# A latent-attention layer in split fp32: scores from two full-height products and one of half height, rotated queries computed in the z stage, a shorter inverse root

## The chip, the cores and the metric

The program runs on one core of a Trainium2 chip. The metric is the device time of one execution in microseconds. Each core has a matrix engine (PE; its weight loads are shown as PEld), a vector engine (DVE), a scalar engine (ACT), GpSimd (POOL) and a queue engine that issues DMAs (SP). The core works from an on-chip memory of 128 partitions; products of PE land in accumulator banks (PSUM), from which DVE and ACT read them.

## The reference, cut to what matters

One layer of multi-head latent attention with a gated output and a per-layer embedding. There are 1024 tokens, 16 heads, 64 plain and 32 rotated query and key features for each head; all heads share one rotated key.

```python
u = h @ w_in
c_q, c_kv, k_rope, z = jnp.split(u, ...)
q = (rmsnorm(c_q, q_norm) @ w_q_b).reshape(B, S, MLA_HEADS, MLA_NOPE + MLA_ROPE)
q_rope = apply_rope(q[..., MLA_NOPE:], cos, sin)
k_rope = apply_rope(k_rope, cos, sin)
s = (einsum('bqhd,bkhd->bhqk', q_nope, k_nope) + einsum('bqhd,bkd->bhqk', q_rope, k_rope)) * scale
prob = softmax(where(k_chunk <= q_chunk, s, -inf))
o = einsum('bhqk,bkhd->bqhd', prob, v)
y = (o * silu(z)) @ w_out
x = x + y
x = x + sigmoid(rmsnorm(x) @ ple_gate) * (p @ ple_proj)
return rmsnorm(x, final_norm)
```

## The kernel before, in words

All values are fp32. PE works on a reduced fp32 form, so each operand is split into a rounded part (`hi`) and the rest (`lo`), and a product is the sum of three: hi·hi, hi·lo and lo·hi. ACT usually makes `hi` by a copy, and DVE or POOL makes `lo` by a subtraction (`sub_hi`, L91).

The stages follow each other. The u stage computes the compressed queries, keys and the raw rotated key for eight tiles of 128 tokens. The z stage (loop over `c`, L513) computes the gate path in eight column blocks of 48 products each; beside it run the last two transposes of u, the rotated key (`rope_key`), the tables of cosines and sines spread over the partitions (`rope_tables`, `cs`) and the query parts of the first four heads (`project_r`). The attention stage loops over 16 heads times 8 blocks of 128 queries in the order `ORDER`; block `i` sees `n = 128 (i+1)` keys. A head has scores (L609), a row maximum on DVE (L614), an exponential on ACT (L619), transposes of the probabilities on PE (L121), the split of these (L650, L91), and the product with the values (L661). Blocks are in flight together: transposes come two blocks behind the scores, values four. For each pair of heads `project_q` and `project_k` (L423, L553) compute queries and keys; for each four heads `project_v` computes values, and `project_r` the query parts that carry the rotation. Calls of these stand at fixed block numbers (`K_AT`, `Q_AT`, `R_AT`, `V_AT`); within them a scheduler sets the order on each engine when the program is built, and engines work in that order. The last stage is the output product, the gate and the embedding (L751), with an inverse root (`rsqrt`, L93) on one column for each tile.

In the scores of before, an array row is one of 128 features: 64 plain ones, 32 query features times cosine, and 32 times sine, against keys arranged to match (`k_hi`, `k_lo`). Each block is three products of the full 128 rows over all its keys, in pieces of up to 512 columns. `project_r` multiplies by the cosine and the sine separately, splits the result and writes both parts to memory outside the core; `rope_q` reads the rows of each head back. The keys of an odd head are copied by DVE to `kst` and split later by ACT and POOL (`odd_k`).

Of the kernel before, what the change touches and what calls it, by code (L numbers as in the profile page):

```python
# [40 lines left out]
V_AT, K_AT, Q_AT, R_AT = (4, 4, 2, 2), (0, 3), (6, 7), (1, 6)  # L41
# [10 lines left out]
def mla_ple_kernel(ctx, tc, x, x_t, p_t, pos, norm_g, w_c, w_z, q_norm, w_q, w_r, kv_norm, w_k, w_v,  # L52
# [338 lines left out]
    cs = [att1.tile([P, S], F32, name=f"cs{e}") for e in range(2)]  # L391
    att2 = late.enter_context(pool("att2", side="right"))
    k_hi, k_lo = zip(*([att2.tile([P, S], F32R, name=f"k_{z}{e}") for z in ("hi", "lo")] for e in range(2)))

    def load_split(src, cols, name, bufs):
# [3 lines left out]
        hi = att1.tile([P, n], F32R, tag=name + "h", name=name + "h", bufs=bufs)  # L399
        lo = att1.tile([P, n], F32R, tag=name + "l", name=name + "l", bufs=bufs)  # L400
        G.tensor_copy(out=hi, in_=stg)
        sub_hi(G, lo, stg, hi)
        return tuple(z.rearrange("p (k n) -> p k n", k=cols[0]) for z in (hi, lo))

    wk_of, wv_of, wq_of, wr_of, q_of, rq_of = {}, {}, {}, {}, {}, {}

    def weights(h):
        if h >= H:
            return
        if h % 4 == 0:  # L410
            wr_of[h // 4] = load_split(w_r[h // 4], (QL // P, P), "wr", 1)
# [15 lines left out]
    def project_r(g, hf):  # L427

        cols = slice(hf * 512, hf * 512 + 512)
        if hf == 0:  # L430
            rq_of[g] = [tc.dram_tile([2, P, S], F32, name=f"rq{g}{z}") for z in "hl"]
        ps = product_q(wr_of[g], hf)
        t = rt_tile("rt").rearrange("p (c n) -> p c n", c=2)
        for n in range(2):
            V.tensor_tensor(out=t[:, n, :], in0=ps, in1=cs[n][:, cols], op=ALU.mult)
        hi = rh_tile("rh").rearrange("p (c n) -> p c n", c=2)
        lo = t.bitcast(F32R)
        A.copy(out=hi, in_=t)
        sub_hi(G, lo, t, hi)
        for z, d in zip((hi, lo), rq_of[g]):  # L440
            nc.gpsimd.dma_start(out=d.rearrange("c p n -> p c n")[:, :, cols], in_=z.bitcast(F32))

    def token_rows(name, src, n):

        blk = rh_tile(name + "b").bitcast(F32)[:, :NT * n]
# [9 lines left out]

    def rope_key():
# [3 lines left out]
        k1, k2 = kr[:, :, :HF], kr[:, :, HF:ROPE]  # L462
        for dst, a, b, op in ((k1, cosT, sinT, ALU.subtract), (k2, sinT, cosT, ALU.add)):
# [3 lines left out]
        V.tensor_copy(out=kr[:, :, ROPE:ROPE + HF], in_=k2)  # L467
        V.tensor_scalar(out=kr[:, :, ROPE + HF:], in0=k1, scalar1=-1.0, scalar2=None, op0=ALU.mult)
        kt = rt_tile("kt")
        d = token_rows("kt", kr, 2 * ROPE)  # L470
        for e in range(2):
            nc.gpsimd.dma_start(out=kt[e * NOPE:(e + 1) * NOPE, :], in_=d)
        for e in range(2):
            rows = slice(NOPE * (1 - e), NOPE * (2 - e))
            A.copy(out=k_hi[e][rows], in_=kt[rows])
            sub_hi(V, k_lo[e][rows], kt[rows], k_hi[e][rows])

    def rope_tables():
        for tab, src, name in zip(cs, (cosT, sinT), ("cos", "sin")):
            t = rt_tile("spread")[:, :NT * 32].rearrange("p (t n) -> p t n", t=NT)  # L480
            V.tensor_copy(out=t.rearrange("p t (m n) -> p t m n", n=HF),
                          in_=src.unsqueeze(2).broadcast_to([P, NT, 32 // HF, HF]))
            d = token_rows(name, t, ROPE)
# [17 lines left out]
    zw = zph.enter_context(pool("zw", reuse_waits="tile"))  # L501

    for c in range(KT):
# [13 lines left out]
        A.activation(out=zT[:, c, :], in_=zT[:, c, :], func=AF.Silu)  # L517
        if c < 2:
            u_transposes(*pend.pop(0))
        if c == 1:  # L520
            rope_key()
        if c == 2:
            rope_tables()
        if c == 3:
            weights(0)
        if c in (4, 5):
            project_r(0, c - 4)
# [14 lines left out]
    kst = att.tile([P, S], F32, name="kst")  # L542
# [4 lines left out]
    def project_k(c, hf):  # L547
# [7 lines left out]
        A.copy(out=k_hi[0][:NOPE, cols], in_=ps[:NOPE])  # L555
        V.tensor_copy(out=kst[NOPE:, cols], in_=ps[NOPE:])
        sub_hi(V, k_lo[0][:NOPE, cols], ps[:NOPE], k_hi[0][:NOPE, cols])
# [20 lines left out]
    def rope_q(h):  # L578
        q_of[h] = [att.tile([P, S], F32R, tag="q" + z, name="q" + z, bufs=3) for z in "hl"]
        r0 = NOPE * (1 - h % 2)  # L580
        for z, d in zip(q_of[h], rq_of[h // 4]):
            for n in range(2):
                nc.sync.dma_start(out=z[r0 + n * ROPE:r0 + (n + 1) * ROPE, :].bitcast(F32),
                                  in_=d[n, h % 4 * ROPE:(h % 4 + 1) * ROPE, :])

    def project_q(c, hf):
        cols = slice(hf * 512, hf * 512 + 512)
        ps = product_q(wq_of[c], hf)
        for e in range(2):
            rows = slice(e * NOPE, (e + 1) * NOPE)  # L590
            hi, lo = q_of[2 * c + e]
            A.copy(out=hi[rows, cols], in_=ps[rows])
            sub_hi(V, lo[rows, cols], ps[rows], hi[rows, cols])
# [302 lines left out]
```

## Time and profile before

| what | value |
|---|---|
| median of 3 runs | 720.14 us (719.3 to 720.26) |
| the profiled execution | 719.65 us |
| its span, first to last instruction | 717.9 us |
| PE busy | 703.2 us (98%), 4032 products |
| DVE busy | 523.8 us (73%) |
| ACT busy | 400.5 us (56%) |
| POOL busy | 214.2 us (30%) |
| granted clock of PE | 0.998 of full speed |

The profiled execution is one run, 1.75 us longer than its span, and 0.49 us below the median. "Busy" counts an instruction from its start to its modelled end, and products of PE overlap, so 98% says that PE is rarely without work, not that it cannot work faster. What a product costs is read from the distance between starts, or from the chain of work, where a row of several products gives their joint length.

### The profile page before, as it was taken

The page shows a single profiled execution, that of the slowest core. Times are in us where ns is not written, and L with a number is a line of the kernel's source. Part 1 is how long each engine was busy: PE and PEld are TensorE (multiplying, and loading weights), DVE is VectorE, ACT ScalarE, POOL GpSimd, SP SyncE. Part 2 cuts the span into 40 slices and gives each one's busy share as a digit, 9 for nine tenths or more (in the row PEclk, how much of TensorE's full clock was granted, in tenths as well). Part 3 has the DMA queues.
Part 4 walks back from the last instruction along what each step waited for, and adds up shares of the span by engine and source line. Part 5 has one row for each costly group of instructions (what it writes and reads, how often), then busy time and mean ns, then how long its engine had stood idle before and what let it go on. Part 6 is the DMA issues. An engine that isn't in the chain of part 4 may idle for free.

```text
span 717.9 us, 11582 instructions
## 1 busy us (share of the span) xinstructions
PE 703.2 (98%) x4032; PEld 612.9 (85%) x4032; DVE 523.8 (73%) x1298; ACT 400.5 (56%) x920; POOL 214.2 (30%) x236
## 2 busy tenths in 40 slices
PE   9999999999999999999999999989999999999995
PEld 7999888888988899889988899878878888888884
DVE  6995553417888888888888888899564168888754
ACT  6752343417777767877767787776353145342322
POOL 0000443214145434554335532264155142000000
PEclk9999999999999999999999999999999999999999
DMA  8720334314103402052211421032573030111101
GB/s 318 279 89 12 122 100 125 103 60 110 38 16 108 147 31 74 1 181 74 66 40 60 136 60 60 15 108 85 179 265 115 1 102 24 38 37 37 60 30 59
DMA packets 26907, 63.95 MB, mean 89 GB/s; under 512 B 4568, under 2 KB 8544, under 8 KB 26848
## 3 DMA queue, kind: packets, MB, share of 16 engines
q1 hardware_dynamic: 23168, 52.19, 22.8%
q0 software_dynamic: 3536, 11.02, 4.6%
q8 instruction: 32, 0.52, 0.3%
q14 instruction: 27, 0.22, 0.1%
q10 hardware_dynamic: 144, 0.00, 0.0%
HBM read 50.01 MB, written 13.18 MB: 88 GB/s over the span
## 4 chain that ended last, share of the span: by engine, by line
PE 90%; DVE 3%; ACT 3%; DMA 2%; issue 1%; POOL 0%; SPq 0%; ACTq 0%; DVEq 0%
PE ps_big L751 21%; PE ps_big L609 13%; PE ps_big L513 12%; PE ps_o L661 10%; PE ps_tr L121 9%; PE ps_pj L423 6%; PE ps_big L215 4%; PE ps_pj L751 3%; PE ps_pj L570 3%; PE ps_pj L553 3%; PE ps_big L216 3%; PE ps_o L215 1%; PE ps_pj L216 1%; DMA wst<-in_w_out 1%; ACT prob L619 1%; PE ps_tr L609 1%
## 5 line engine op out<-in xcount | busy, mean ns | idle before, releaser
L751 PE MATMUL ps_big<-w,aTh 128*128 128x512 f32 (+1 forms) x480 | 139.0, 390 | 0.0
L751 PEld LDWEIGHTS ps_big<-w,aTh 128*128 128x128 f32 x480 | 89.4, 188 | 20.2
L619 ACT ACTIVATE prob<-ps_big,mx 128x384 f32<-128x384 f32 (+6 forms) x112 | 89.4, 798 | 16.2 <-DVE mx L614 15.5
L614 DVE TENSOR_REDUCE mx<-ps_big 128x1 f32<-128x384 f32 (+6 forms) x112 | 91.6, 818 | 1.8
L121 PE MATMUL ps_tr<-ident,prob 128*128 128x128 f32 x576 | 84.1, 273 | 2.0 <-ACT prob L619 2.0
L751 PE MATMUL ps_big<-w,aTl 128*128 128x512 f32 (+1 forms) x240 | 84.6, 390 | 0.0
L121 PEld LDWEIGHTS ps_tr<-ident,prob 128*128 128x128 f32 x576 | 68.3, 140 | 11.7 <-ACT prob L619 2.8
L91 DVE TENSOR_TENSOR pt8l<-ps_tr,pt8h 128x512 fp32r<-128x512 f32 (+3 forms) x128 | 71.0, 582 | 4.5 <-ACT pt8h L650 3.8
L667 POOL TENSOR_TENSOR zT<-o,zT 64x256 f32<-64x256 f32 x56 | 41.1, 736 | 94.2 <-DVE o L665 80.6
L609 PE MATMUL ps_big<-k_hi,qh 128*128 128x512 f32 (+2 forms) x176 | 67.7, 385 | 0.9 <-ACT prob L619 0.8
L650 ACT CAST pt8h<-ps_tr 128x512 fp32r<-128x512 f32 (+3 forms) x128 | 60.7, 509 | 4.7 <-PE ps_tr L121 4.3
L609 PE MATMUL ps_big<-k_lo,qh 128*128 128x512 f32 (+2 forms) x176 | 62.0, 352 | 0.0
L609 PE MATMUL ps_big<-k_hi,ql 128*128 128x512 f32 (+2 forms) x176 | 61.4, 349 | 0.0
L661 PE MATMUL ps_o<-pt8h,vals 128*128 128x256 f32 x224 | 57.6, 294 | 0.0
L661 PE MATMUL ps_o<-pt8l,vals 128*128 128x256 f32 x224 | 55.0, 282 | 0.0
L751 PEld LDWEIGHTS ps_big<-w,aTl 128*128 128x128 f32 x240 | 45.0, 188 | 10.2 <-POOL aTl L91 0.5
L116 ACT ACTIVATE jk<-xs 128x512 bf16<-128x512 f32 (+2 forms) x25 | 18.8, 751 | 45.2 <-DVE xs L829 37.3
L661 PEld LDWEIGHTS ps_o<-pt8l,vals 128*128 128x128 f32 x224 | 42.9, 191 | 0.0
L661 PEld LDWEIGHTS ps_o<-pt8h,vals 128*128 128x128 f32 x224 | 42.6, 190 | 0.0
L650 ACT CAST pt4h<-ps_tr 128x384 fp32r<-128x384 f32 (+3 forms) x64 | 27.2, 426 | 27.3 <-PE ps_tr L121 27.1
L360 ACT ACTIVATE zh<-zs,g_col 128x128 fp32r<-128x128 f32 x56 | 18.3, 392 | 42.1 <-DMA zs<-in_w_z 36.1
L609 PEld LDWEIGHTS ps_big<-k_hi,qh 128*128 128x128 f32 x176 | 33.2, 189 | 7.7 <-ACT prob L619 3.5
(285 smaller groups left out, 1740.2 us busy)
## 6 DMA issues: line engine op xcount, KB each, us to landing
zT<-in_x SPq DMA_DIRECT2D x8, 512.0 KB, 5.0
rlb<-rl SPq DMA_DIRECT2D x32, 128.0 KB, 3.1
wst<-in_w_out SPq DMA_DIRECT2D x8, 512.0 KB, 4.4
xs<-in_x SPq DMA_DIRECT2D x8, 512.0 KB, 7.2
wst<-in_ple_gate SPq DMA_DIRECT2D x8, 512.0 KB, 4.0
out<-xs SPq DMA_DIRECT2D x16, 256.0 KB, 2.0
zs<-in_w_z SPq DMA_DIRECT2D x14, 256.0 KB, 2.9
zT<-in_x_t SPq DMA_DIRECT2D x6, 512.0 KB, 4.1
```

Source lines behind the costliest of these rows:

```text
L91: eng.tensor_tensor(out=lo, in0=src, in1=hi.bitcast(F32), op=ALU.subtract)
L121: nc.tensor.transpose(dst[:, j * P:(j + 1) * P], src[:, j * P:(j + 1) * P], ident)
L215: nc.tensor.matmul(pq, st, mv[:, k, :QL], start=first, stop=last)
L423: nc.tensor.matmul(ps, w[b][:, k, :], (cq_hi, cq_lo)[a][:, k, hf * 512:hf * 512 + 512], start=k == 0 and a + b == 0, stop=k == n - 1 and a ...
L513: nc.tensor.matmul(ps[:, hf * 512:(hf + 1) * 512], wz[b][:, k % 4, :], (hT_hi, hT_lo)[a][:, k, hf * 512:(hf + 1) * 512], start=k == 0 and ...
L609: nc.tensor.matmul(ps[:, off + s0:off + s1], q[a][:, qs], (k_hi, k_lo)[b][e][:, s0:s1], start=a + b == 0, stop=a == 1)
L614: V.tensor_reduce(out=mx, in_=s, axis=AX.X, op=ALU.max, negate=True)
L619: A.activation(out=pr[:, :n], in_=s, func=AF.Exp, bias=mx, scale=1.0, accum_out=l)
L650: A.copy(out=hi[:, j0:j0 + n, half], in_=src)
L661: nc.tensor.matmul(ps[:, :256], w, z[:, j, :], start=j + n == 0, stop=j == last and n == 1)
L667: (V if h >= H - 2 else G).tensor_tensor(out=z, in0=o[top], in1=z, op=ALU.mult)
L751: nc.tensor.matmul(o, st[a][:, k, :], w[k][b][:, cols], start=k == 0 and a + b == 0, stop=k == nk - 1 and a == 1)
```

## The change

**Scores.** A query tile `q1` (`qa`) now holds 64 rounded plain features, 32 rounded rotated features and the rests of these 32; `k1` holds the rounded plain keys and the rounded rotated key twice. A second tile `q2` (`qb`) holds the rests of the plain features and a copy of the rounded ones, against `k2` (rounded plain keys and their rests). The third product needs only the rotated half: 64 rows of `q1` against `kr_lo`, the rests of the rotated key. From 512 keys up, all three products are made in two halves of the columns, each half in a PSUM bank of its own, and the third product of the second half takes its 64 rows from another tile, `q3`, in the other half of the array. Below 512 keys there is one piece, and one product of 64 rows. The row maximum and the exponential read both banks in one instruction.

**Rotation.** `project_r` computes the rotated query itself (four DVE operations in place of two, an ACT copy and a DVE subtraction of half the size in place of ones of the full size) for all four groups of four heads, in z blocks 2 to 5, with its weights split by ACT and DVE. `rope_tables` moves from block 2 to block 0, the first attention weights from block 3 to 6.

**Copies.** `project_q` and `project_k` gain POOL copies of 64 x 512; `odd_k` runs on POOL alone, with two copies of 64 x 1024 and the subtraction. `kr_lo` is made by DVE at the start of the attention. `project_q` now runs its second half of the columns first (`Q_AT`), and `rope_q` is issued at block 1 of an odd head in place of block 6.

**Inverse root and end.** `rsqrt` has one operation less at its start and another form of one operation in each of its three steps. The last tile's output is written in four parts of 256 columns, two from ACT and two from DVE, one of them through ACT's queue.

```diff
-V_AT, K_AT, Q_AT, R_AT = (4, 4, 2, 2), (0, 3), (6, 7), (1, 6)
+V_AT, K_AT, Q_AT, ROPE_AT = (4, 4, 2, 2), (0, 3), (7, 6), 1
...
-        half = small.tile([P, n], I32, tag=f"rs_i{n}", name="rs_i", bufs=2)
-        V.tensor_scalar(out=half, in0=v.bitcast(I32), scalar1=1, scalar2=None,
-                        op0=ALU.logical_shift_right)
...
-        V.tensor_scalar(out=y.bitcast(I32), in0=half, scalar1=-1, scalar2=0x5F3759DF,
+        V.tensor_scalar(out=y.bitcast(I32), in0=v.bitcast(I32), scalar1=-0.5, scalar2=0x5F3759DF,
                         op0=ALU.mult, op1=ALU.add)
...
-                V.tensor_scalar(out=t, in0=y, scalar1=y, scalar2=h, op0=ALU.mult, op1=ALU.mult)
+                V.scalar_tensor_tensor(out=t, in0=y, scalar=y, in1=h, op0=ALU.mult, op1=ALU.mult)
...
+        ps = product_q(wr, hf)
+        (t0, t1), (hi, lo) = (z.rearrange("p (c n) -> c p n", c=2) for z in (t, u))
+        V.tensor_tensor(out=t0, in0=ps, in1=cs[0][:, cols], op=ALU.mult)
+        top, bot = slice(0, NOPE), slice(NOPE, P)
+        V.tensor_tensor(out=t1[bot], in0=ps[top], in1=cs[1][top, cols], op=ALU.mult)
+        V.scalar_tensor_tensor(out=t1[top], in0=ps[bot], scalar=-1.0, in1=cs[1][bot, cols],
+                               op0=ALU.mult, op1=ALU.mult)
+        V.tensor_tensor(out=t0, in0=t0, in1=t1, op=ALU.add)
+        hi = hi.bitcast(F32R)
+        A.copy(out=hi, in_=t0)
+        sub_hi(V, lo.bitcast(F32R), t0, hi)
...
+        if 2 <= c < 6:
+            project_r(c - 2, wr, 0, zT[:, 6, :], zT[:, 7, :])
+            project_r(c - 2, wr, 1, rt_tile("rt"), rh_tile("rh").bitcast(F32))
+            if c < 5:
+                wr = weights_r(c - 1)
...
-        A.copy(out=k_hi[1][NOPE:], in_=kst[NOPE:])
-        sub_hi(G, k_lo[1][NOPE:], kst[NOPE:], k_hi[1][NOPE:])
+        top, bot = slice(0, NOPE), slice(NOPE, P)
+        G.tensor_copy(out=k1[1][bot], in_=kst[0][bot])
+        sub_hi(G, k2[1][top], kst[0][bot], k1[1][bot])
+        G.tensor_copy(out=k2[1][bot], in_=kst[0][bot])
...
+            A.copy(out=qa[rows, cols], in_=ps[rows])
+            sub_hi(V, qb[rows, cols], ps[rows], qa[rows, cols])
+            G.tensor_copy(out=qb[other, cols], in_=qa[rows, cols].bitcast(F32))
...
-        for s0, s1 in spans:
-            for a, b in pairs:
-                nc.tensor.matmul(ps[:, off + s0:off + s1], q[a][:, qs], (k_hi, k_lo)[b][e][:, s0:s1],
-                                 start=a + b == 0, stop=a == 1)
...
+        if n < 512:
+            m = max(n, 256)
+            parts = [(ps[:, :m], slice(0, m), qa, rope)]
+            s, masked = ps[:, :n], ps[0:64, n - 64:n]
+        else:
+
+            s = ps.rearrange("p (b n) -> p b n", b=2)[:, :, :w]
+            parts = [(s[:, 0, :], slice(0, w), qa, rope), (s[:, 1, :], slice(w, n), qc, nope)]
+            masked = s[0:64, 1, w - 64:]
+        for q, k in ((qa, k1[e]), (qb, k2[e])):
+            for o, cols, _, _ in parts:
+                nc.tensor.matmul(o, q[:, qs], k[:, cols], start=q is qa, stop=False)
+        for o, cols, q, rows in parts:
+            nc.tensor.matmul(o, q[rows, qs], kr_lo[rows, cols], start=False, stop=True)
...
-                if h % 4 == 2 and h + 2 < H and at in R_AT:
-                    project_r(h // 4 + 1, R_AT.index(at))
...
+        for i, cols in enumerate([slice(z, z + 256) for z in range(0, D, 256)] if last else halves):
```

How the order on the engines moves is seen at three places. The first is PE in head 1, the block of 896 keys: in each row stands the source line, the accumulator, and after the arrow the keys and the queries. Before:

```order
L609 MATMUL ps_big_2204<-k_hi1_989,qh_1744 128x512
L609 MATMUL ps_big_2204<-k_lo1_990,qh_1744 128x512
L609 MATMUL ps_big_2204<-k_hi1_989,ql_1745 128x512
L609 MATMUL ps_big_2204<-k_hi1_989,qh_1744 128x384
L609 MATMUL ps_big_2204<-k_lo1_990,qh_1744 128x384
L609 MATMUL ps_big_2204<-k_hi1_989,ql_1745 128x384
```

The same block in the changed kernel, with the transposes of an earlier block ahead of it:

```order
L118 MATMUL ps_tr_2337<-ident_61,prob_2268 128x128 x3
L633 MATMUL ps_big_2343<-k11_969,q1_1853 128x448 x2
L633 MATMUL ps_big_2343<-k21_970,q2_1854 128x448 x2
L635 MATMUL ps_big_2343<-kr_lo_1842,q1_1853 128x448
L635 MATMUL ps_big_2343<-kr_lo_1842,q3_1848 128x448
```

Six products of 128 rows have become four of 128 rows (448 columns each) and two of 64 rows that stand next to each other.

The second place is PE in head 6, at the block of 640 keys. Before, the nine products of `project_r` (`wrh`, `wrl`) follow its scores:

```order
L609 MATMUL ps_big<-k_hi_987,qh 128x256
L609 MATMUL ps_big<-k_lo_988,qh 128x256
L609 MATMUL ps_big<-k_hi_987,ql 128x256
L423 MATMUL ps_pj<-cq_hi,wrh 128x512
L423 MATMUL ps_pj<-cq_hi,wrl 128x512
L423 MATMUL ps_pj<-cq_lo,wrh 128x512
...
L121 MATMUL ps_tr<-ident,prob 128x128 x2
```

Now the scores are followed by transposes at once:

```order
L633 MATMUL ps_big<-k_967,q_3376 128x320 x2
L633 MATMUL ps_big<-k_968,q_3377 128x320 x2
L635 MATMUL ps_big<-kr_lo,q_3376 128x320
L635 MATMUL ps_big<-kr_lo,q_3378 128x320
L118 MATMUL ps_tr<-ident,prob 128x128 x2
L686 MATMUL ps_o<-pt8h,vals 128x256
```

So heads 2, 6 and 10 have no projection left between their scores, transposes and values; the 54 products concerned stand in z now.

The third place is POOL at the change from an odd to an even head, with what each row waits for. Before:

```order
L91 TENSOR_TENSOR k_lo_990<-kst,k_hi_989 64x1024 [waits Activation_49]
L401 CAST wqh<-ws 128x384 [waits DMAHW5_49,PE_49,Pool_49]
L91 TENSOR_TENSOR wql<-ws,wqh 128x384 [waits Pool_49]
L667 TENSOR_TENSOR zT<-o_2919,zT 64x256 [waits DVE_49,Pool_49]
L667 TENSOR_TENSOR zT<-o_2976,zT 64x256 [waits DVE_49]
```

The same place now (`k_969` and `k_970` are `k1` and `k2` of the odd heads, `q_3377` and `q_3384` are `q2` of the next two heads):

```order
L609 CAST q_3377<-q_3376 64x512 [waits Activation_49]
L573 CAST k_969<-kst 64x1024 [waits PE_49]
L575 CAST k_970<-kst 64x1024 [waits PE_49]
L609 CAST q_3384<-q_3383 64x512 [waits Activation_49]
L91 TENSOR_TENSOR k_970<-kst,k_969 64x1024 [waits Pool_49]
L609 CAST q_3377<-q_3376 64x512 [waits Activation_49]
L400 CAST wqh<-ws 128x384 [waits DMAHW4_49,PE_49,Pool_49]
L91 TENSOR_TENSOR wql<-ws,wqh 128x384 [waits Pool_49]
L609 CAST q_3384<-q_3383 64x512 [waits Activation_49,Pool_49]
L692 TENSOR_TENSOR zT<-o_3637,zT 64x256 [waits DVE_49]
```

Six copies have come in, and the copy of `q2` that the next head needs stands behind the odd keys.

## Rows read from the trace of the kernel before

**Rows 1.** The page, its head and busy time by engine.
```profile
span 717.9 us, 11582 instructions
PE 703.2 (98%) x4032; PEld 612.9 (85%) x4032; DVE 523.8 (73%) x1298; ACT 400.5 (56%) x920; POOL 214.2 (30%) x236
```
**Rows 2.** The page, chain of work that ended last, shares by engine and line.
```profile
PE 90%; DVE 3%; ACT 3%; DMA 2%; issue 1%; POOL 0%; SPq 0%; ACTq 0%; DVEq 0%
PE ps_big L751 21%; PE ps_big L609 13%; PE ps_big L513 12%; PE ps_o L661 10%; PE ps_tr L121 9%; PE ps_pj L423 6%; PE ps_big L215 4%; PE ps_pj L751 3%; PE ps_pj L570 3%; PE ps_pj L553 3%; PE ps_big L216 3%; PE ps_o L215 1%; PE ps_pj L216 1%; DMA wst<-in_w_out 1%; ACT prob L619 1%; PE ps_tr L609 1%
```
**Rows 3.** Windows: z, heads 0 to 13, heads 14 and 15; us, busy by engine, clock, DMA.
```profile
69.00:161.40 92.40, 92.40 (x414) 76.33 (x413) 39.02 (x103) 32.71 (x79) 29.41 (x42) 1.00 0.34 101
...
169.50:466.30 296.80, 296.79 (x1999) 269.44 (x2000) 255.62 (x549) 223.40 (x536) 121.72 (x128) 1.00 0.23 69
466.30:506.80 40.50, 36.76 (x252) 32.06 (x250) 36.70 (x79) 28.37 (x72) 20.43 (x14) 1.00 0.29 88
```
**Rows 4.** The chain in order of time, one pair of heads: start, length, what.
```profile
282.70 1.40 PE ps_big L609 x6
...
284.43 1.22 PE ps_big L609 x6
...
287.52 0.35 PE ps_tr L609 x3
...
291.19 2.07 PE ps_pj L423 x9
```
**Rows 5.** Timeline of PE and PEld, three products of one block: start, length, instruction.
```profile
282.54 0.39 PE L609 MATMUL ps_big<-k_hi,qh 128*128 128x512 f32 x1
282.54 0.19 PEld L609 LDWEIGHTS ps_big<-k_lo,qh 128*128 128x128 f32 x1
...
282.77 0.39 PE L609 MATMUL ps_big<-k_lo,qh 128*128 128x512 f32 x1
282.77 0.19 PEld L609 LDWEIGHTS ps_big<-k_hi,ql 128*128 128x128 f32 x1
```
**Rows 6.** The chain in order of time, seven transposes in a row.
```profile
293.26 0.76 PE ps_tr L121 x7
```
**Rows 7.** Timeline of PE round a product with 16 stationary columns.
```profile
218.68 0.27 PE L628 MATMUL ps_tr<-ident,rl 128*16 128x128 f32 x1
...
218.71 0.48 PE L609 MATMUL ps_big<-k_lo,qh 128*128 128x512 f32 x1
```
**Rows 8.** Windows, a pair of heads with the two halves of project_r.
```profile
294.98:336.94 41.96, 41.96 (x275) 37.59 (x274) 36.29 (x78) 31.92 (x75) 20.98 (x22) 1.00 0.34 109
```
**Rows 9.** Groups of DVE by shape in the window of rows 8.
```profile
L435 DVE TENSOR_TENSOR rt<-ps_pj,cs 128x512 f32<-128x512 f32 x4 | 2.6, 683 | 0.7 <-PE ps_pj L423 0.7
```
**Rows 10.** Groups of POOL by shape, whole span.
```profile
L91 POOL TENSOR_TENSOR k_lo<-kst,k_hi 64x1024 fp32r<-64x1024 f32 x8 | 19.2, 2400 | 24.4 <-PE ps_pj L423 20.8 <-ACT k_hi L561 3.5
...
L401 POOL CAST wvh<-ws 128x512 fp32r<-128x512 f32 x4 | 2.4, 612 | 10.9 <-DMA ws<-in_w_v 10.9
```
**Rows 11.** Timeline of DVE in head 14.
```profile
481.03 2.37 DVE L667 TENSOR_TENSOR zT<-o,zT 64x256 f32<-64x256 f32 x1
```
**Rows 12.** The chain in order of time at the start of the attention.
```profile
168.88 0.59 ACT qh L592
...
169.51 0.73 PE ps_big L609 x2
```
**Rows 13.** Groups of DVE by shape: rest of the rotated key.
```profile
L91 DVE TENSOR_TENSOR k_lo<-kt,k_hi 64x1024 fp32r<-64x1024 f32 x2 | 2.4, 1220 | 3.0 <-ACT k_hi L475 3.0
```
**Rows 14.** The chain in order of time, end of the program.
```profile
711.15 0.15 DVE rs_i L96
...
711.53 0.28 DVE rs_t L106
...
711.83 0.17 DVE r L107
...
713.10 0.72 ACT xs L841
```

More of the change, by code (lines that the diff above doesn't have):

```diff
@@ L390, in mla_ple_kernel, with load_split @@
     att1 = late.enter_context(pool("att1", side="right"))
-    cs = [att1.tile([P, S], F32, name=f"cs{e}") for e in range(2)]
     att2 = late.enter_context(pool("att2", side="right"))
-    k_hi, k_lo = zip(*([att2.tile([P, S], F32R, name=f"k_{z}{e}") for z in ("hi", "lo")] for e in range(2)))
-    def load_split(src, cols, name, bufs):
+    k1, k2 = zip(*([att2.tile([P, S], F32R, name=f"k{z}{e}") for z in (1, 2)] for e in range(2)))
+    def load_split(src, cols, name, bufs, home=att1, copy=G.tensor_copy, eng=G):
         n = math.prod(cols)
@@ L425, in product_q, with project_r, token_rows @@
         return ps
-    def project_r(g, hf):
+    def project_r(g, wr, hf, t, u):
+        if hf == 0:
+            rq_of[g] = tc.dram_tile([2, P, S], F32, name=f"rq{g}")
         cols = slice(hf * 512, hf * 512 + 512)
[L430 to L445, printed above, removed]
+        ps = product_q(wr, hf)
[9 more added lines that the diff above has]
+        sub_hi(V, lo.bitcast(F32R), t0, hi)
+        nc.gpsimd.dma_start(out=rq_of[g].rearrange("z p s -> p z s")[:, :, cols],
+                            in_=u.rearrange("p (c n) -> p c n", c=2))
+    def token_rows(name, src, blk, n):
         V.transpose(out=blk, in_=src.rearrange("p t n -> p (t n)"))
@@ L474, in rope_key @@
             rows = slice(NOPE * (1 - e), NOPE * (2 - e))
-            A.copy(out=k_hi[e][rows], in_=kt[rows])
-            sub_hi(V, k_lo[e][rows], kt[rows], k_hi[e][rows])
+            A.copy(out=k1[e][rows], in_=kt[rows])
+        return d
     def rope_tables():
-        for tab, src, name in zip(cs, (cosT, sinT), ("cos", "sin")):
-            t = rt_tile("spread")[:, :NT * 32].rearrange("p (t n) -> p t n", t=NT)
+        for n, (tab, src, name) in enumerate(zip(cs, (cosT, sinT), ("cos", "sin"))):
+            t, blk = zT[:, 2 + n, :256].rearrange("p (t n) -> p t n", t=NT), zT[:, 2 + n, 256:512]
             V.tensor_copy(out=t.rearrange("p t (m n) -> p t m n", n=HF),
                           in_=src.unsqueeze(2).broadcast_to([P, NT, 32 // HF, HF]))
-            d = token_rows(name, t, ROPE)
+            d = token_rows(name, t, blk, ROPE)
             for i in range(4):
@@ L501, in mla_ple_kernel, with weights_r @@
     zw = zph.enter_context(pool("zw", reuse_waits="tile"))
+    cs = [zw.tile([P, S], F32, name=f"cs{e}") for e in range(2)]
+    def weights_r(g):
+        return load_split(w_r[g], (QL // P, P), "wr", 1, zw, A.copy, V)
     for c in range(KT):
@@ L520, in mla_ple_kernel @@
         if c == 1:
[L521 to L524, printed above, removed]
+            key_rows = rope_key()
+        if 2 <= c < 6:
[3 more added lines that the diff above has]
+                wr = weights_r(c - 1)
+        if c == 6:
             weights(0)
-        if c in (4, 5):
-            project_r(0, c - 4)
+            kt = rh_tile("kt").bitcast(F32)
+            for e in range(2):
+                nc.gpsimd.dma_start(out=kt[e * NOPE:(e + 1) * NOPE, :], in_=key_rows)
     zph.close()
@@ L589, in project_q @@
         for e in range(2):
[L590 to L593, printed above, removed]
+            rows, other = slice(e * NOPE, (e + 1) * NOPE), slice((1 - e) * NOPE, (2 - e) * NOPE)
+            qa, qb = q_of[2 * c + e]
+            A.copy(out=qa[rows, cols], in_=ps[rows])
+            sub_hi(V, qb[rows, cols], ps[rows], qa[rows, cols])
+            G.tensor_copy(out=qb[other, cols], in_=qa[rows, cols].bitcast(F32))
     def order(h):
@@ L618, in scores @@
         l = sums[h // 2][:, e * NT + i:e * NT + i + 1]
-        A.activation(out=pr[:, :n], in_=s, func=AF.Exp, bias=mx, scale=1.0, accum_out=l)
+        to = pr[:, :n] if n < 512 else pr[:, :n].rearrange("p (b n) -> p b n", b=2)
+        A.activation(out=to, in_=s, func=AF.Exp, bias=mx, scale=1.0, accum_out=l)
         return pr
@@ L667, in values @@
         (V if h >= H - 2 else G).tensor_tensor(out=z, in0=o[top], in1=z, op=ALU.mult)
+    kr_lo = att.tile([P, S], F32R, name="kr_lo")
+    for e in range(2):
+        rows = slice(NOPE * (1 - e), NOPE * (2 - e))
+        sub_hi(V, kr_lo[rows], kt[rows], k1[e][rows])
     A.activation(out=warm[:, 1:], in_=zT[:, KT - 1, S - 1:], func=AF.Exp, scale=0.0)
@@ L673, in mla_ple_kernel @@
         project_k(0, hf)
+    for hf in (1, 0):
         project_q(0, hf)
@@ L704, in mla_ple_kernel @@
                     project_q((h + 1) // 2, Q_AT.index(at))
-                if h % 2 and at == Q_AT[1]:
+                if h % 2 and at == max(Q_AT):
                     weights(h + 3)
@@ L837, in mla_ple_kernel @@
         r = rsqrt(ms[:, i:i + 1], 1, name="r3", bufs=2)
-        for hf in range(2):
-            cols = halves[hf]
-            if last and hf == 0:
+        for i, cols in enumerate([slice(z, z + 256) for z in range(0, D, 256)] if last else halves):
+            on_act = last and i < 2
+            if on_act:
                 A.activation(out=xs[:, t, cols], in_=xs[:, t, cols], func=AF.Copy, scale=r)
@@ L844, in mla_ple_kernel @@
                                        in1=f_bc[:, cols], op0=ALU.mult, op1=ALU.mult)
-            nc.sync.dma_start(out=out[t * P:(t + 1) * P, cols], in_=xs[:, t, cols])
+            (nc.scalar if on_act and i else nc.sync).dma_start(out=out[t * P:(t + 1) * P, cols], in_=xs[:, t, cols])
 def kernel(**inputs):
```

61 lines of the change are left out of this document (32 added, 29 removed).

## The prediction

> **What bounds the kernel now.** I read the page first, then the chain, then windows by stage. On the page PE is busy 98% of the 717.9 us and no other engine over 73% [rows 1]; the chain that ended last lies on PE for 90% of its length [rows 2]. The reader is to see that a change pays only where it shortens PE's own work or a stall of PE. The windows say where PE has stalls: in z and in heads 0 to 13 it is busy throughout, while DVE has 255.62 of 296.80 us in the latter; in heads 14 and 15 PE has 36.76 of 40.50 us, so there something else ends last [rows 3]. The granted clock is 1.00 in all three stretches, the level of 2.4 GHz, so it gives nothing to either side.
>
> "Busy" hides that products overlap, so I take prices from the chain. Six products of 512 columns take 1.40 us, 0.233 each. A block of 896 keys (three of 512 and three of 384) takes 1.22, so one of 384 columns takes (1.22 - 3 x 0.233) / 3 = 0.174. Three of 256 take 0.35, 0.117 each [rows 4]. These lie on a line of 0.453 ns a column, which gives 0.146 for 320 and 0.204 for 448 columns.
>
> **The change: scores.** Before, one full pass over the eight blocks of a head is 256 columns twice (0.234), 384 (0.174), 512 (0.233), 640 (0.174 + 0.117), 768 (0.233 + 0.117), 896 (0.233 + 0.174) and 1024 (0.466): 2.155 us, and 6.465 us for the three products. For 16 heads that is 103.4 us; the chain has 13% and 1% of the span on this line, some 100 us [rows 2].
>
> Now two full passes cost 0.408 for the small blocks and 2 x (0.117 + 0.146 + 0.174 + 0.204 + 0.233) = 1.748 for the split ones, so 4.312 in all. The third product of the small blocks has 64 rows and as many columns as before: 0.408, if rows don't matter. What is left is five pairs of half-height products, and no row of before shows such a pair. Its bounds: one after the other, 1.748 a head, and the gain is nothing (6.468 against 6.465); fully side by side, 0.874, and the gain is 0.871 us a head.
>
> Between these stands the loading of weights. Each load starts at the start of the product ahead of it, never earlier [rows 5]: a load needs that product to have begun. Seven transposes take 0.76 us, 0.109 each [rows 6], with a load for each, so two loads one behind the other need some 0.218. If both loads of a pair can run while the product of `q2` ahead of them streams, that product's start and the end of the second load are 0.218 apart. The pair is then done 0.218 after that earlier product for 256 to 448 columns, and 0.233 after it for 512, against twice the column time. The five pairs cost 4 x 0.218 + 0.233 = 1.105, and the gain is 0.64 us a head. If the second load starts only when the first half-product has begun, as a literal reading of the loads has it [rows 5], each pair costs its column time and 0.109: 1.419, a gain of 0.33. I take 0.64: what the loads show is met by it too, since the two loads go to different halves of the array, and it lies between the ends.
>
> I count it for 14 heads: 9.0 us. In heads 14 and 15 PE waits for the others already, so less PE work is worth nothing there; one reason is DVE's gate product of 2.37 us for 64 x 256, far longer than most of its kind [rows 11]. The change doesn't touch it.
>
> **Rotation.** Six halves of `project_r`, nine products of some 2.07 us together [rows 4], leave the attention and enter z: 12.4 us from one stage that PE bounds to another, so the sum is nothing. The cover in z: DVE is busy 39.02 of 92.40 us and ACT 32.71 [rows 3]. Each half costs DVE five operations of 0.69 at most (683 ns for 128 x 512 [rows 9]), so eight cost 27 us, less the 3 us there now; with the weights' subtractions z has some 65 us of DVE work in 105. If that cover were gone, the next gate block would wait, but it has a second PSUM buffer, a block of 11 us ahead. The earlier tables, the late `weights(0)` and `kt` stand on POOL's queue and SP's, in z, a block or more ahead of their users: nothing.
>
> **Heads without a projection.** Moving it has a price. A pair of heads takes 41.96 us with 36.29 us of DVE [rows 8]. Four DVE products of 683 ns leave [rows 9], so some 33.6 us remain. PE keeps 41.96 - 4.2 - 1.3 = 36.5. DVE is then at 92%, and heads 2, 6 and 10 have no filler for PE. In heads 14 and 15 DVE is at 36.70 of 40.50, 91%, and PE lost 3.7 us in two heads, though with that long gate product. I put 0.3 us on each of the three heads, 0.9 (bounds: 0 and 1.9 each, so 0 to 5.6).
>
> **Copies on POOL.** A copy of 64 x 512 is at most the 0.612 of 128 x 512; one of 64 x 1024 I put at twice that, 1.2; the subtraction takes 2.4 [rows 10]. Behind the last score of an odd head POOL must do two long copies, a `q2` copy, the subtraction and the next `q2` copy: 1.2 + 1.2 + 0.6 + 2.4 + 0.6 = 6.0 us. The consumer is the third block of the next head. Until then PE has a half of `project_q` (2.1), transposes, values and two blocks, over 8 us: hidden by 2. POOL's gate products behind it come later by as much, and ACT's copies of the output, which wait for them, have two buffers. Nothing, and up to 1 us a pair if that cover fails.
>
> **Start of the attention.** Before, the first score starts at 169.51, behind ACT's query copy [rows 12]. Now DVE makes `kr_lo` ahead of its key copies: 2 x 1.22 = 2.4 us [rows 13], of which some two thirds fall into time in which DVE waited for ACT. PE comes to the scores earlier, since ten value products have moved behind the first. I put 0.5 us (0 to 2.4).
>
> **End.** `rs_i` takes 0.15 of the chain; the three `rs_t` go from 0.28 to about the 0.17 of their neighbour `r` [rows 14]: 0.15 + 0.33 = 0.48. The last part of the output is a quarter of a row in place of half: 0.72 [rows 14] becomes about two steps of 0.4, of which the first part's DMA hides one, and one DMA goes by ACT's queue. I put 0.5 for it (0 to 0.6). Together 1.0.
>
> **Sum.** -9.0 + 0.9 + 0.5 - 1.0 = -8.6. The profiled execution took 719.65 us; that makes 711.05, and with its 0.49 us under the median, **711.5 us**.
>
> **Rivals.**
>
> *Pairs fully side by side.* The gain is 14 x 0.871 = 12.2, the sum -11.8: **708.3**. For it: the two halves use different rows, keys and banks, and nothing says that two loads to different halves must queue [rows 5]. Against it: the 0.109 of a load [rows 6], and heads at 92% of DVE. The page "TensorE: Matmul & The Clock Gate" of the Trainium skill (part 3, "The mechanism") says that products in different row groups start about 4 ns apart and that their loads overlap; by that rule this rival holds. No row here shows it.
>
> *Second load late.* 14 x 0.33 = 4.6, the sum -4.2: **715.9**. For it the literal reading of the loads [rows 5].
>
> *No overlap.* The change would not do what it says: the pairs run one after the other, and PE's slack in the heads stays, so no 0.9: 0 + 0.5 - 1.0 = -0.5, or **719.6**. For it only that no row shows two products at once.
>
> *The array empties at each change of height.* Every block goes from 128 rows to 64 and back, 256 changes in 128 blocks. If the next product may start only when the one before has left the array, each costs up to 0.39 - 0.23 = 0.16 us, the part of a product that now lies beside its successor [rows 5]: 41 us, against 12 at best, so some **749**, slower. It decides from 8.6 / 256 = 0.034 us a change. For it: a product is in flight 0.16 us after the next begins, and nothing shows a change of height. Against it: the one product whose shape differs, with 16 stationary columns, is followed by the next after 0.03 us [rows 7], but it has 128 rows. The page "TensorEngine Tiling (Array Packing)" of the Trainium skill (section "Key Properties") says that a change of tiling mode drains TensorE; by that rule this rival holds, and no run here shows it yet.
>
> **How the numbers follow.** Forecast 0.32, fully side by side 0.24, late load 0.15, no overlap 0.10, emptying 0.19. The forecast's own range is 709.5 to 714, from 0 to 5.6 for the bare heads and the bounds of start and end, little of their far ends. The range for 8 in 10 takes in all but the emptying: 707.0 to 720.5. A measurement of this kernel can tell about 0.2%, 1.4 us, from no change. Faster: the first three and some of the fourth, 0.73; same: most of the fourth and an emptying that happens to cancel, 0.08; slower: 0.19.
>
> **What the profile will show.** Starts of the two 64-row products: under 0.02 us apart for the rival, up to 0.1 for 256 columns and 0 for 512 for the forecast, 0.109 throughout for the late load, a column time for no overlap. An emptying shows as a gap ahead of the first 64-row product and ahead of the product behind the second. Such pairs of heads [rows 8] should take 36.5 to 37 us, z some 105. The prediction is wrong if PE has waits for DVE or ACT of over 2 us in heads 2, 6 and 10, if POOL's copies appear as releasers of scores, or if a pair costs more than two column times.

## The result and the profile after

The changed kernel took 756.16 us (median of 4 runs, 755.92 to 757.95), the kernel before 719.72 us beside it. The ratio is 1.0514, with a 95% interval of 1.0498 to 1.0529: 36 us slower, where 8.6 us faster had been forecast. The profiled execution took 755.92 us, 36.3 more than the one of before.

The head of the page and the groups of PE that hold 64-row products:

```profile
span 754.1 us, 11689 instructions
PE 737.2 (98%) x4080; PEld 609.4 (81%) x4080; DVE 543.3 (72%) x1301; ACT 392.2 (52%) x917; POOL 229.6 (30%) x278
...
L635 PE MATMUL ps_big<-kr_lo,q 64*128 64x384 f32 (+2 forms) x192 | 51.6, 434 | 0.9 <-DMA q<-rq 0.9
...
L635 PE MATMUL ps_tr<-kr_lo,q 64*128 64x256 f32 x16 | 6.1, 381 | 0.0
```

PE is still busy 98%, as in [rows 1], and the span is 36.2 us longer: PE itself became slower, no other engine took over. Windows of the changed kernel (columns as in [rows 3]): z, start of the attention, the 16 heads, the rest. They begin and end at the same points of the program as 69.00, 161.40, 169.50 and 506.80 us of before.

```profile
70.60:175.65 105.05, 105.05 (x467) 86.46 (x466) 60.66 (x135) 37.45 (x89) 21.25 (x34) 1.00 0.39 117
175.65:185.30 9.65, 6.99 (x31) 5.45 (x29) 9.08 (x11) 5.81 (x9) 7.07 (x13) 1.00 0.09 35
185.30:543.25 357.95, 354.29 (x2252) 287.56 (x2252) 285.76 (x614) 239.00 (x593) 155.35 (x176) 1.00 0.15 51
543.25:754.10 210.85, 202.06 (x910) 164.35 (x908) 133.98 (x318) 72.50 (x139) 38.85 (x24) 0.99 0.24 80
```

Against [rows 3], z is longer by 12.65 us, the 12.4 of the moved rotation and little else; the start by 1.55 (it was 161.40 to 169.50, 8.10); the rest shorter by 0.25 (it was 717.9 - 506.80 = 211.10); and what lies ahead of z by 1.6, which runs of the old code show too (below). The heads took 337.30 and take 357.95, although 12.4 us of work have left them: 33 us have come in, all of it with PE busy.

The timeline shows where. Rows of PE and its loads in head 5, a block of 512 keys between products of `project_k`: start, length, instruction.

```profile
347.26 0.63 PE L633 MATMUL ps_big<-k,q 128*128 128x256 f32 x4
347.82 0.38 PE L635 MATMUL ps_big<-kr_lo,q 64*128 64x256 f32 x2
348.14 0.50 PE L560 MATMUL ps_pj<-ckv_lo,wkh 128*128 128x512 f32 x1
348.47 0.39 PE L560 MATMUL ps_pj<-ckv_hi,wkh 128*128 128x512 f32 x1
348.70 0.40 PE L560 MATMUL ps_pj<-ckv_hi,wkl 128*128 128x512 f32 x1
...
347.04 0.65 PEld L633 LDWEIGHTS ps_big<-k,q 128*128 128x128 f32 x4
347.82 0.19 PEld L635 LDWEIGHTS ps_big<-kr_lo,q 64*128 64x128 f32 x2
348.14 0.19 PEld L560 LDWEIGHTS ps_pj<-ckv_lo,wkh 128*128 128x128 f32 x1
348.25 0.19 PEld L560 LDWEIGHTS ps_pj<-ckv_hi,wkh 128*128 128x128 f32 x1
```

Read it by distances. The two 64-row products take 0.38 together, the length of one: they run fully side by side (their starts are 3 ns apart in the records). But the pair starts 0.09 late, since four products of 0.117 from 347.26 end at 347.73. The next product starts 0.32 behind the pair, not 0.12, and the one after it 0.33 behind that, not 0.23; only then the rhythm of 0.23 is back. The loads say why. Among products of one height a load runs beside the product ahead of it, as in [rows 5]; at a change of height it starts with its own product (347.82 and 348.14 stand in both lists), so it is hidden behind nothing.

A visit is one stretch of 64-row products, a pair or a single one, between products of 128 rows. The 128 blocks make 135 visits, since in seven of the blocks of 768 keys other products stand between the two of a pair; 73 of the 80 pairs run side by side. Over all visits of the trace the distances, worked out from the starts of products (us, medians), are:

| columns of the first product | 128 to 128 rows | 128 to 64 | 64 (one or a pair) to 128 |
|---|---|---|---|
| 256 | 0.119 | 0.209 | 0.311 |
| 320 | 0.147 | 0.239 | 0.343 |
| 384 | 0.175 | 0.267 | 0.370 |
| 448 | 0.204 | 0.297 | 0.395 |
| 512 | 0.231 | 0.327 | 0.430 |

The way in costs 0.09 at any width, the way out 0.19, and the second product behind it another 0.10 (0.056 where that is a transpose, 80 times). The sums are 12.3, 26.2 and 9.4 us, together 47.9. The pairs save 12.5. That leaves 35.4, where 33 us have come into the heads: the distances count some 2 us too much, and where they do is not shown. The rest of the 36.3 us is the start of the attention and what lies ahead of z.

Waits of PE for others (total, times, longest): the two longest that were not there before. Both are at the start of the attention.

```profile
PE ps_big L633 <- DVE q L91: 2.7, 1, 2.7
...
PE ps_big L635 <- DMA q<-rq: 0.9, 1, 0.9
```

### The profile page after: what moved, and what is told of

The parts are those of the page before. It is cut to its first block, busy times and chain, and to the rows that moved or that the text cites. A ratio compares the mean times of both kernels' runs of the same rounds, so it can differ in the third digit from the quotient of the medians.

```text
span 754.1 us, 11689 instructions
## 1 busy us (share of the span) xinstructions
PE 737.2 (98%) x4080; PEld 609.4 (81%) x4080; DVE 543.3 (72%) x1301; ACT 392.2 (52%) x917; POOL 229.6 (30%) x278
## 5 line engine op out<-in xcount | busy, mean ns | idle before, releaser
L633 PE MATMUL ps_big<-k,q 128*128 128x384 f32 (+4 forms) x384 | 91.3, 350 | 3.1 <-DVE q L91 2.7
L118 PE MATMUL ps_tr<-ident,prob 128*128 128x128 f32 x576 | 89.4, 281 | 1.4 <-ACT prob L644 1.4
L118 PEld LDWEIGHTS ps_tr<-ident,prob 128*128 128x128 f32 x576 | 63.7, 140 | 20.8 <-issue 8.0
L633 PEld LDWEIGHTS ps_big<-k,q 128*128 128x128 f32 x384 | 61.1, 190 | 8.2 <-ACT q L607 3.1
L635 PE MATMUL ps_big<-kr_lo,q 64*128 64x384 f32 (+2 forms) x192 | 51.6, 434 | 0.9 <-DMA q<-rq 0.9
L635 PEld LDWEIGHTS ps_big<-kr_lo,q 64*128 64x128 f32 x192 | 22.0, 183 | 27.9 <-issue 21.8
L690 DVE TENSOR_TENSOR o<-ps_o,o 64x256 f32<-64x256 f32 x64 | 26.8, 419 | 13.6 <-ACT o L689 12.9
```

The source lines that it names most:

```text
L118: nc.tensor.transpose(dst[:, j * P:(j + 1) * P], src[:, j * P:(j + 1) * P], ident)
L633: nc.tensor.matmul(o, q[:, qs], k[:, cols], start=q is qa, stop=False)
L635: nc.tensor.matmul(o, q[rows, qs], kr_lo[rows, cols], start=False, stop=True)
L690: V.tensor_tensor(out=o[top], in0=ps[top, :256], in1=o[top], op=ALU.add)
```

## The experiments

Theory A: each visit to a product of 64 rows costs PE some 0.35 us, by its two changes of height, whatever stands around it. Rivals: B, the cost lies in the rest of the change; C, 64-row products are themselves slow; D, it is the price of running two halves at once.

**Full height.** The third product on 128 rows, with zeros in the half of the keys without rotation; `q3` and its reads go with it:

```diff
-        for o, cols, q, rows in parts:
-            nc.tensor.matmul(o, q[rows, qs], kr_lo[rows, cols], start=False, stop=True)
+        for o, cols, _, _ in parts:
+            nc.tensor.matmul(o, qa[:, qs], kr_lo[e][:, cols], start=False, stop=True)
```

> The third product has all 128 rows again (the 64 rows that carry no rotated feature meet zeros in two key tiles, both column parts take the same query tile), so no product of the scores changes height and nothing runs side by side; all else is as in the changed kernel. Theory A (each visit to 64 rows costs PE time): the trace of the changed kernel has 135 visits, with 12.4 us of excess at the way in, 27.0 us at the way out and some 9.4 us on the second product behind, 48.8 us in all, less 12.5 us that the pairs save, so 36 us go: 719 to 722 us, equal to the kernel before within 0.3%. Rival B (the cost is in the rest: rotation in z, copies on POOL, heads without a projection): it stays above 740 us. If A holds, what is left between this kernel and the one before is the sum of my other terms (bare heads +0.9, start +0.5, end -1.0: +0.4).

Measured: 727.01 us, 1.0102 of before (1.0086 to 1.0119). 29 us went, which B can't explain; but 719 to 722 had been expected, and 7.6 us over the kernel before (719.43 beside it) remain, where my other terms sum to +0.4. Its largest wait of PE is at the first score, and is taken up below:

```profile
PE ps_big L631 <- DMA q<-rq: 3.4, 1, 3.4
```

The stall has a second price. Behind it the granted clock is 0.50, the level of 1.2 GHz, and products of 256 columns stand 0.21 apart in place of 0.12. One window of it (the clock is the third number from the end):

```profile
186.20:187.20 1.00, 1.00 (x7) 1.00 (x6) 0.97 (x3) 0.00 (x0) 1.00 (x1) 0.50 0.13 53
```

The rows stay low from 185.2 to 188.4 us, so some 1.6 us are lost (an estimate: half of this time). In the changed kernel PE idles for 2.7 us at this place, and the clock stays at 1.00.

**Both products in one half.** The second column part takes `q1` in place of `q3`, whose reads are gone too:

```diff
-            parts = [(s[:, 0, :], slice(0, w), qa, rope), (s[:, 1, :], slice(w, n), qc, nope)]
+            parts = [(s[:, 0, :], slice(0, w), qa, rope), (s[:, 1, :], slice(w, n), qa, rope)]
```

> Both 64-row products of a block take the same query tile and so the same half of the array; nothing else changes. Theory A: as many visits as in the changed kernel, but the second product starts a column time (0.119 to 0.231 us) behind the first in place of 0.003: +12.5 to 14 us, 768.5 to 770 us. Rival C (a 64-row product is itself as slow as its distance to the next one suggests, 0.31 to 0.43 us): 80 pairs by some 0.37 us, +29 us, 785 us. Rival D (the price is one of running two halves at once): the time falls below 756 us.

Measured: 765.77 us (one run), +9.6, short of the 12.5 to 14 expected. From the end of z to the last score its trace takes 11.3 us more than the changed kernel's; ahead of z this run is 1.5 us the faster one, which has nothing to do with the scores, and behind its stall of 3.5 us at the first score its clock is low for some 3 us. So the overlap is real and worth about this much; D falls, and C with it. Timeline of a block of 768 keys:

```profile
326.21 0.61 PE L633 MATMUL ps_big<-kr_lo,q 64*128 64x384 f32 x2
326.75 0.33 PE L118 MATMUL ps_tr<-ident,prob 128*128 128x128 f32 x1
```

Two 64-row products one behind the other take 0.54 to the next start. Two visits at the 0.370 of the table would be 0.74: the second product of a visit is no visit of its own.

**The old kernel with one short product.** Nothing of the change but the height of the last of three products:

```diff
+                r = slice(0, 64 if a else P)
-                nc.tensor.matmul(ps[:, off + s0:off + s1], q[a][:, qs], (k_hi, k_lo)[b][e][:, s0:s1],
+                nc.tensor.matmul(ps[:, off + s0:off + s1], q[a][r, qs], (k_hi, k_lo)[b][e][r, s0:s1],
```

> The kernel before, with the last of the three products of each piece of the scores made on rows 0 to 63 alone (half of the sum over features of that product is left out). Nothing else of the change is in it. There are 176 such products, each between two of 128 rows. Theory A, with the three excesses of the changed kernel's trace (0.091 in, 0.194 out, 0.103 or, where a transpose follows, 0.056 on the second behind): 0.34 to 0.39 us a visit, +60 to +68 us, 780 to 788 us. Rivals B and D (other parts of the change, or pairs): 720 us. My prediction's bound of 0.16 us a change would give 176 x 0.32 = +56 us, 776 us.

Measured: 783.57 us (one run), +64.1. There are 192 such products (16 more than I counted, in the blocks of 128 keys), so 0.334 us a visit. Timeline of one block, products and loads:

```profile
282.41 0.48 PE L610 MATMUL ps_big<-k_hi,qh 128*128 128x512 f32 x1
282.73 0.39 PE L610 MATMUL ps_big<-k_lo,qh 128*128 128x512 f32 x1
283.05 0.50 PE L610 MATMUL ps_big<-k_hi,ql 64*128 64x512 f32 x1
283.48 0.50 PE L610 MATMUL ps_big<-k_hi,qh 128*128 128x512 f32 x1
283.82 0.39 PE L610 MATMUL ps_big<-k_lo,qh 128*128 128x512 f32 x1
...
283.05 0.18 PEld L610 LDWEIGHTS ps_big<-k_hi,ql 64*128 64x128 f32 x1 [0.36 <-issue]
283.48 0.19 PEld L610 LDWEIGHTS ps_big<-k_hi,qh 128*128 128x128 f32 x1 [0.25 <-issue]
283.59 0.19 PEld L610 LDWEIGHTS ps_big<-k_lo,qh 128*128 128x128 f32 x1
```

Distances of 0.32, 0.43 and 0.34 stand where 0.233 is normal. The idle time of the loader ahead of a change (0.36 and 0.25) is the load that could not run ahead. This kernel also has z starting late, by 1.9 us (the changed one by 1.6), though all ahead of its scores is the old code. In both, PE works at about half its rate up to some 10 us after the beginning: a product of 288 columns is followed after 0.24 us (8.77 to 9.01 in the changed kernel, 8.83 to 9.07 here), where the kernel before has 0.13 (8.50 to 8.63). Five of the twelve traces, of both kinds of code, begin z late like this, and seven do not. So this part of the difference is not the change's, and a single run can carry up to 1.9 us of it.

**Fewer visits.** The changed kernel with full height in the blocks under 512 keys (`if n < 512:` the product of the first experiment).

> The changed kernel, with the third product at 128 rows in the blocks of under 512 keys (two small key tiles with zeros) and as changed in the others. Theory A: 48 visits fewer of some 0.36 us, -17 us: 738 to 741 us; and the pairs that remain don't pay for themselves, so it stays some 18 us over the kernel with full height throughout (80 visits x 0.37 less 12.5). Rival B: no change, 756 us.

Measured: 742.79 us (one run, with a late z), a little over the range expected. 13.4 us went with 48 visits, and it is 15.8 above full height throughout: the 87 visits that remain in its trace cost more than their pairs save.

**Other heights.** The third experiment with 96 and with 32 rows, and with 64 rows in two of three products:

```diff
-                r = slice(0, 64 if a else P)
+                r = slice(0, 96 if a else P)
...
+                r = slice(0, 32 if a else P)
...
+                r = slice(0, 64 if a or b else P)
```

> The kernel before, with the last of the three products of each piece made on rows 0 to 95 in place of 0 to 127 (a quarter of the sum over features of that product is left out). Reading 1 (every change of the number of rows empties the array): as with 64 rows, 783 us. Reading 2 (only a change to a part of half the array or less does; 96 rows count as the whole array): 720 us. No row so far tells them apart; I give each a half.

> The kernel before, with the last of the three products of each piece made on rows 0 to 31 (three quarters of the sum over features of that product are left out). With 64 rows the 192 such products cost 64 us, with 96 rows nothing. Reading 1 (a change to half of the array or less costs one price, whatever the part): 783 to 784 us. Reading 2 (the price grows with the part of the array that is left out): over 800 us.

> The kernel before, with the second and the third product of each piece on rows 0 to 63 (half of the sum over features of both is left out): 384 products of 64 rows, but as many visits to 64 rows as with one, 192. Theory A (a price for each visit: 0.091 ahead of the first product of the new height and 0.103 ahead of its second, at either change): the 0.103 ahead of the second now falls on the second 64-row product, the sum stays: 783 to 786 us. Rival C (a price for each 64-row product): twice the 64 us, 847 us.

Measured: 719.33 us with 96 rows (before 719.78), 783.39 with 32, 784.64 with two short products (each one run; before 721.04 beside the last two). So 96 rows cost nothing, and the price is that of a visit, not of the rows left out, nor of each product. Timelines, first with 96 rows, then with two products of 64:

```profile
282.85 0.40 PE L610 MATMUL ps_big<-k_lo,qh 128*128 128x512 f32 x1
283.08 0.40 PE L610 MATMUL ps_big<-k_hi,ql 96*128 96x512 f32 x1
283.32 0.39 PE L610 MATMUL ps_big<-k_hi,qh 128*128 128x512 f32 x1
```

```profile
283.04 0.49 PE L610 MATMUL ps_big<-k_lo,qh 64*128 64x512 f32 x1
283.38 0.39 PE L610 MATMUL ps_big<-k_hi,ql 64*128 64x512 f32 x1
283.70 0.50 PE L610 MATMUL ps_big<-k_hi,qh 128*128 128x512 f32 x1
284.13 0.50 PE L610 MATMUL ps_big<-k_lo,qh 64*128 64x512 f32 x1
```

With 96 rows the rhythm stays at 0.23. With two short products, the first of each height is longer by its own load (0.49 and 0.50 against 0.39), and what follows it pays 0.10: a change has the same two parts in either direction.

**The reads of the rotated rows.** In the full-height kernel and in the changed one, each read of a head's 32 rows is cut in two:

```diff
-                nc.sync.dma_start(out=z[r0 + n * ROPE:r0 + (n + 1) * ROPE, :].bitcast(F32),
-                                  in_=rq_of[h // 4][n].rearrange("(c h n) s -> h c n s", c=2, h=4)[h % 4])
+                for x in range(2):
+                    r, d = r0 + n * ROPE + x * HF, x * NOPE + h % 4 * HF
+                    nc.sync.dma_start(out=z[r:r + HF, :].bitcast(F32), in_=rq_of[h // 4][n, d:d + HF, :])
```

> The kernel with full height throughout, whose reads of a head's 32 rotated rows (two groups of 16 rows, 64 rows apart, in one DMA of 128 KB) are each cut into two DMAs of 16 neighbouring rows. In its trace the first score waits 3.4 us for such a read, and the DMAs move some 50 GB/s there, a tenth of the engines being busy, where the kernel before moves over 200 GB/s. Theory E (one DMA with two groups of rows goes by two of the 16 engines, and the late read makes the late start of the attention): the reads land within 4 us and the start comes earlier by 1 to 3.4 us (DVE's subtraction for the queries is next): 724 to 726 us. Rival F (DVE's two subtractions for the rest of the rotated key ahead of its key copies make the late start): no change, 727 us.

> The changed kernel itself with the same cut of the reads. Theory E: the one wait of 0.9 us of a 64-row product for a read goes, and of the 2.7 us that the first score waits the part that the read makes: 753.5 to 755.5 us. Rival F: 0.9 us at most, 755.3 us.

Measured: full height with two reads 722.81 us, 1.0043 of before (1.0028 to 1.0058), 4.2 less than without and 1.2 below the range expected; the changed kernel with two reads 756.03 us, no difference, where 753.5 to 755.5 had been expected. Windows at the start of the attention, 178 to 184 us, of the changed kernel, then of full height with two reads, and that one's issues (count, size, us to landing):

```profile
178.00:184.00 6.00, 4.64 (x21) 3.52 (x19) 5.67 (x8) 4.34 (x8) 5.25 (x7) 1.00 0.11 44
```

```profile
178.00:184.00 6.00, 5.22 (x30) 4.43 (x28) 5.65 (x9) 4.42 (x9) 5.68 (x8) 1.00 0.49 142
...
q<-rq SPq DMA_DIRECT2D x64, 64.0 KB, 2.2
```

The last two columns are the DMA's busy share and GB/s. With one read of two groups of 16 rows 0.11 of the 16 engines is busy, 1.8 engines, and 44 GB/s move; with reads of 16 neighbouring rows it is 0.49 and 142. The page "DMA: Bandwidth & Descriptors" of the Trainium skill (section "Rules for kernel authors") says that an outermost dimension of size c under 16 holds a whole DMA to at most c engines; here c is 2, and the trace agrees. Which engines they are the trace does not show. So theory E holds for full height, F doesn't. From the last product of z to the last score the two full-height traces differ by 3.7 us (334.2 and 330.4): the stall of 3.4 has become one of 0.8, and the clock stays at 1.00. The rest of the 4.2 is not the reads' by these traces; the one without two reads has another wait of 1.6 in the last stage, for ACT. In the changed kernel the read was repaired as well and nothing came of it: products of the values moved ahead of the first score, and as much time is lost 8 us behind it, where a score waits for an accumulator that the exponential still holds:

```profile
PE ps_big L634 <- ACT prob L645: 2.9, 2, 2.6
```

Behind this stall of 2.6 us the clock is low again, up to 198.2 us:

```profile
195.00:196.00 1.00, 1.00 (x6) 1.00 (x7) 0.67 (x2) 0.00 (x0) 0.00 (x0) 0.50 0.06 16
```

A stall of 2.7 us had left it at 1.00 in the changed kernel; the traces don't show what decides.

**The end alone.** The kernel before with the shorter `rsqrt` and the four parts of the last output, as in the diff ahead of the prediction.

> The kernel before with two parts of the change alone: the shorter inverse root and the last tile's output in four parts. My prediction's term: -1.0 us (0.48 for the root, 0.5 for the output; bounds 0 to 1.1), so 718.4, a ratio of 0.9986. Rival: nothing that can be measured, as the trace of the changed kernel has 8.50 us from the last product's start to the end against 8.82 before, only 0.3 us less: ratio 0.9996.

Measured: 718.60 us, 0.9983 of before (0.9972 to 0.9994). This is the one version that beats the kernel before, by 1.2 us. Its profile, of its fastest run, has only 0.3 us less behind the last product (8.51 against 8.82); the rest lies in the heads, whose instructions stand in the same order as before, and I have no cause for it. The chain of the changed kernel at the end (start, length, what) explains the 0.3:

```profile
747.75 0.15 DVE r L96
...
748.00 0.23 DVE rs_t L103
...
749.40 0.07 ACT xs L869
749.47 0.34 issue
749.81 0.49 ACT xs L869
```

Beside [rows 14], `rs_i` is gone, but an `rs_t` fell from 0.28 to 0.23 and not to 0.17, and the two quarters on ACT take 0.90 with what lies between them, where one half took 0.72.

## Why the prediction was wrong

**The step that failed** is the price of the third product: "0.408, if rows don't matter", and the pairs costed by their columns and loads alone. Rows matter when they change. The price for each visit, from the times of the runs:

| comparison | visits | time between, us | overlap lost, us | us a visit |
|---|---|---|---|---|
| old kernel, 64 rows | 192 | 64.1 | 0 | 0.334 |
| old kernel, 32 rows (before taken at 719.7) | 192 | 63.7 | 0 | 0.332 |
| old kernel, 64 rows twice (the same) | 194 | 64.9 | 0 | 0.335 |
| changed against full height | 135 | 29.2 | 12.5 | 0.309 |
| the same, two reads in both | 135 | 33.2 | 12.3 | 0.337 |
| large blocks only, against full height | 87 | 15.8 | 12.5 | 0.325 |

Against the one run of before beside them, 721.04 us, the second and third rows give 0.325 and 0.328; without the 1.9 us of its late z the first gives 0.324. So each of the 135 visits cost 0.31 to 0.34 us, 42 to 46 us together, against 12.5 that the pairs saved: this turned a gain into a loss. The prediction had named this as a sign of being wrong: a pair of 256 columns took 0.31 to the next product, more than two column times, 0.23.

The price stood among the rivals with 0.19: "up to 0.39 - 0.23 = 0.16 us" a change is 0.32 a visit, and both of its signs came, a gap ahead of the first 64-row product and one ahead of the product behind. That the size fits so well is in part luck: a change is not one gap of 0.16 but 0.09 ahead of the first product and 0.10, or 0.06 at a transpose, ahead of the second, whose load came late. Its 749 us fell 7 us short: 14 more changes than 256 are 2.2 us, the start 1.55, the time ahead of z 1.6; the rest is open. What I weighed wrongly was the evidence: the row that spoke against it [rows 7] has a product of 128 rows and so no change of height, as I wrote beside it. Nor does its 0.03 say much: the next product starts at 219.02, so the two take 0.34, the sum of their usual 0.109 and 0.231.

```profile
219.02 0.40 PE L609 MATMUL ps_big<-k_hi,ql 128*128 128x512 f32 x1
```

The page "TensorEngine Tiling (Array Packing)" of the Trainium skill (section "Key Properties") says that a change of tiling mode drains TensorE. The runs fit this, with 0.31 to 0.34 us a visit, though that the array empties is not seen itself; they add that 96 rows bring no change and that the load at the change is exposed too.

**Overlap.** The forecast had 0.64 us a head. Full overlap came, the rival's 0.871 a head. That its 14 x 0.871 = 12.2 lies so near to the trace's 12.5 is chance: the saving came in all 16 heads, less the seven pairs that were split. The loads of the pair don't queue, two take 0.19 together (at 347.82 above). The page "TensorE: Matmul & The Clock Gate" of the Trainium skill (part 3, "The mechanism") says that loads to different row groups overlap, and the trace agrees.

**Start of the attention.** +0.5 (0 to 2.4) was too small: the stretch is 1.55 longer, and the waits are 2.7 and 0.9, the second of them behind its end. I looked at DVE's subtractions and counted the reads at nothing, without a reason. Without visits the slow read was worth 3.7 us, the low clock behind its stall included.

**Rotation.** 12.65 us came into z, against 12.4 counted as moved: right. z took the 105 us that I gave. **Bare heads.** With full height and two reads a pair of heads takes 38.43, and PE is busy for 38.23:

```profile
216.75:255.18 38.43, 38.23 (x263) 34.88 (x262) 34.08 (x74) 28.79 (x72) 19.39 (x24) 1.00 0.13 37
```

That is 3.53 less than [rows 8], where 4.14 of products left: +0.6 a pair, within the bounds of 0 to 1.9, above the 0.3 taken. In the changed kernel itself PE was too slow for this to show. **Copies on POOL.** None is a releaser of a score in any of these traces: right. **End.** -1.0 in the sum and -1.2 (-2.0 to -0.4) by itself, but not by the terms I named.

What stays open: 3.0 us between full height with two reads and the kernel before. By stages of its profile they lie at the start of the attention (+1.9, of which 0.8 is a wait), ahead of z (+0.7), in z and the heads together (+0.9) and in the rest (-0.4).

## What to carry to other kernels

Before products are cut to half the array's height, count the changes of height, not the rows saved: each visit costs 0.31 to 0.34 us here, and a pair of 512-column products side by side gives back at most 0.23. By these numbers it pays only where one visit holds several pairs, which no run tried; 96 rows in place of 128 cost nothing and give nothing. When the layout of a buffer outside the core changes, look at the outermost dimension of its reads before counting them as hidden. And a stall of PE can cost more than its length: read the granted clock behind it. Where versions are measured once, look how much of a difference lies in stages that the edit doesn't touch.

## What the hardware did that I had not expected

A change between 128 rows and 64 or fewer has two parts in either direction: 0.09 us ahead of the first product of the new height, and 0.10 ahead of its second, because the first one's load is not run ahead. Reads of 128 KB in two groups of 16 rows kept 1.8 of 16 engines busy, several of them in the queue. Half-height products in different halves start 3 ns apart. And in four of the versions the granted clock was 0.50 behind a stall of PE of 2.6 to 3.5 us at the scores, while in the changed kernel it stayed at 1.00 behind 2.7 us.
